# Gated DeltaNet in a fused encoder layer: a 64-row inverse applied twice, front results in DRAM, two fronts per inverse, loads and stores in program order

## The chip, the cores and the metric

The kernel runs on one core of one Trainium2 chip. The metric is the device time of one execution in microseconds (us). All matrices are float32; the large products are made from two exact parts of each operand (a rounded high part and a low rest), three matmuls for one product.

## The reference, cut to what matters

One layer: RMS norm of 1104 tokens (16 meta tokens, 64 of a sample stream, 1024 of a prompt), an input projection of 2048 to 8208 columns, two mixers, an output projection, the residual and a final norm. The mixer that the change touches is the gated DeltaNet, 8 heads of 128, in chunks:

```python
kk = einsum('nbhid,nbhjd->nbhij', kc * bc[..., None], kc) * decay
a_mat = where(strict, kk, 0.0) + eye
t_mat = triangular_solve(a_mat, eye, left_side=True, lower=True, unit_diagonal=True)
u = einsum('nbhij,nbhjd->nbhid', t_mat, vc * bc[..., None])
w = einsum('nbhij,nbhjd->nbhid', t_mat, kc * (bc * exp(gc))[..., None])
# per chunk, in order
v_new = u_i - einsum('bhcd,bhde->bhce', w_i, s)
o = einsum('bhcd,bhde->bhce', q_i * exp(g_i)[..., None], s) + einsum('bhij,bhje->bhie', qk_i, v_new)
s = s * exp(g_last)[..., None, None] + einsum('bhcd,bhce->bhde', k_i * exp(g_last[..., None] - g_i)[..., None], v_new)
```

## The kernel before

The tokens lie in three pieces of 336, 384 and 384 columns. The input projection goes through 64 tiles of 128 output channels, one *job* each. For a tile the weights come in four *chunks* of 256 KB (`Weights`: `load` on the SyncE queue into `wr`, `split` into `wh` on ScalarE and `wl` on VectorE); a chunk feeds 36 matmuls, four groups of nine (three pieces, three products), all into the PSUM tiles `pj`. The first 24 jobs take one piece each; the other 56 take all three pieces, in the order of the string `order` (L416): `b0` is the four tiles (K, Q, V, Z) of head 0, `a2` four tiles of the other mixer. After a tile its convolution, SiLU and gate go on beside the next tile (`convs`), and K, Q, V and Z of a head go to scratch tensors `scr` in DRAM.

The DeltaNet runs beside the projections too. Its unit is three chunks of 128 tokens of one head, 24 units in all, each with a *front* and a *back*. `dn_front` (L717) loads K and Q, transposes them on TensorE (`psq`, `psk`) for the norms, forms the decays, and makes with three matmuls `psm` the masked triangle `bm` and the attention `at`. It stores `bm` to `e_in`; GpSimd loads the twelve 32x32 blocks on the diagonals as 12 rows of `eT`, inverts them with 30 pairs of TENSOR_TENSOR (L792, L794), stores them to `e_out` and loads them back as `t32`. `dn_back` (L803) joins two and two blocks of 32 to 64 (`psx`, `psy`), then the two of 64 to one inverse of 128 (the 64x64 matmuls named `psy2`, `psx2`, `psy3` in the code; they stand as psy and psx with 64*64 in the rows), transposes the values (`psv`), and then takes the three chunks in order: `psr` (keys times state), `r` on VectorE, `psu` (inverse times r), `u` on ScalarE, `psn` (the new state), two matmuls into `po`, `sn` on VectorE. At the end the norm, a transpose (`pot`), the gate, and a store to `yscr`.

The order of the program follows a planner: `clk` adds up the work of TensorE, VectorE and ScalarE, and after each group of nine matmuls `pump` (L182) takes one stage more of whatever is ready; each `yield` gives the planned wait until the next stage. An inverse is planned at `EL` = 5 + 50 of the planner's us. VectorE runs in the order in which the program is written; a scheduler sets the order of the other engines and of the SyncE queue. Every queue takes its instructions strictly in order, so a DMA that waits for its data holds what stands behind it. All matmuls of the helper `mm` have line L83, all VectorE and ScalarE work of the wrapper `Timed` L61.

## Time and profile before

| | us |
|---|---|
| median of 3 runs | 2288.12 |
| lowest and highest run | 2285.22, 2289.0 |
| span of the profiled execution | 2283.8 |
| TensorE busy in that span | 2211.3 (97%) |
| VectorE, ScalarE, GpSimd busy | 1335.5, 640.1, 940.4 |

The profiled execution gives its span from the first to the last instruction; the runs' times hold in addition what lies around it, so the median stands 4.3 us above the span. The profile's page says first how long each engine was busy; then, slice by slice, where; then the chain of work that ended last. A busy share of 97% says that most of what can be won is work taken off TensorE or the little time in which it waits.

### The profile page before, as it was taken

The page shows a single profiled execution, that of the slowest core. Times are in us where ns is not written, and L with a number is a line of the kernel's source. Part 1 is how long each engine was busy: PE and PEld are TensorE (multiplying, and loading weights), DVE is VectorE, ACT ScalarE, POOL GpSimd, SP SyncE. Part 2 cuts the span into 40 slices and gives each one's busy share as a digit, 9 for nine tenths or more (in the row PEclk, how much of TensorE's full clock was granted, in tenths as well). Part 3 has the DMA queues.
Part 4 walks back from the last instruction along what each step waited for, and adds up shares of the span by engine and source line. Part 5 has one row for each costly group of instructions (what it writes and reads, how often), then busy time and mean ns, then how long its engine had stood idle before and what let it go on. Part 6 is the DMA issues. An engine that isn't in the chain of part 4 may idle for free.

```text
span 2283.8 us, 36007 instructions
## 1 busy us (share of the span) xinstructions
PE 2211.3 (97%) x12938; PEld 2074.7 (91%) x12938; DVE 1335.5 (58%) x3421; ACT 640.1 (28%) x1575; POOL 940.4 (41%) x1557
## 2 busy tenths in 40 slices
PE   7799999999999999999999999999999999999998
PEld 6699889999999999999999999999999997788886
DVE  7964355667576547655664567456645345464544
ACT  5443122222222222222222222122222125444341
POOL 4520006657466645555665666655464300000000
PEclk9999999999999999999999999999999999999999
DMA  6444223232323222322222222222222238654652
GB/s 224 148 154 142 64 65 90 69 95 70 91 84 91 71 76 81 97 64 77 80 78 73 79 81 86 73 61 83 86 80 63 62 97 279 216 192 153 217 175 83
DMA packets 168790, 242.69 MB, mean 106 GB/s; under 512 B 18332, under 2 KB 92260, under 8 KB 168484
## 3 DMA queue, kind: packets, MB, share of 16 engines
q1 hardware_dynamic: 163076, 228.84, 32.1%
q0 software_dynamic: 3072, 7.11, 1.7%
q10 hardware_dynamic: 2464, 4.46, 0.5%
q8 instruction: 101, 1.65, 0.3%
q14 instruction: 77, 0.63, 0.1%
HBM read 196.14 MB, written 44.17 MB: 105 GB/s over the span
## 4 chain that ended last, share of the span: by engine, by line
PE 82%; DVE 11%; DMA 2%; issue 2%; ACT 2%; POOL 0%; SPq 0%; DVEq 0%; ACTq 0%; POOLq 0%
PE pj L83 58%; PE po L83 16%; DVE acc L61 2%; PE psy L83 2%; DVE wl L61 2%; DMA yr<-yscr 1%; PE psx L83 1%; PE psm L83 1%; PE psn L83 1%; PE pjb L83 1%; PE psu L83 1%; PE psr L83 1%; ACT jk L61 1%; DVE rot L61 1%; DVE xl L61 1%
## 5 line engine op out<-in xcount | busy, mean ns | idle before, releaser
L83 PE MATMUL pj<-xh,wh 128*128 128x384 f32 x2048 | 692.9, 338 | 8.0 <-DVE raw L61 3.5
L83 PE MATMUL pj<-xl,wh 128*128 128x384 f32 x2048 | 690.6, 337 | 1.1 <-DVE xl L61 1.1
L83 PE MATMUL pj<-xh,wl 128*128 128x384 f32 x2048 | 690.5, 337 | 0.5 <-DVE wl L61 0.4
L61 DVE TENSOR_TENSOR wl<-wr,wh 128x512 fp32r<-128x512 f32 x496 | 371.2, 753 | 343.3 <-ACT wh L61 341.7
L83 PE MATMUL pj<-x,wh 128*128 128x320 f32 (+3 forms) x2048 | 530.6, 340 | 9.4 <-ACT x L61 6.5
L61 ACT CAST wh<-wr 128x512 fp32r<-128x512 f32 x496 | 305.3, 618 | 719.1 <-PE pj L83 522.8
L792 POOL TENSOR_TENSOR tm<-eT 12x30 f32<-12x30 f32 (+4 forms) x720 | 392.1, 545 | 127.3 <-DMA eT<-e_in 72.8
L794 POOL TENSOR_TENSOR eT<-eT,tm 12x30 f32<-12x30 f32 (+4 forms) x720 | 418.5, 581 | 56.4
L83 PEld LDWEIGHTS pj<-xh,wh 128*128 128x128 f32 x2048 | 385.4, 188 | 12.7 <-issue 4.0
L83 PEld LDWEIGHTS pj<-xl,wh 128*128 128x128 f32 x2048 | 385.1, 188 | 2.1 <-DVE xl L61 1.7
L83 PEld LDWEIGHTS pj<-xh,wl 128*128 128x128 f32 x2048 | 384.9, 188 | 1.4 <-DVE wl L61 1.4
L83 PEld LDWEIGHTS pj<-x,wh 128*128 128x128 f32 x2048 | 353.7, 193 | 21.1 <-ACT x L61 6.5
L83 PE MATMUL pj<-x,wl 128*128 128x320 f32 (+3 forms) x1024 | 324.0, 316 | 11.0 <-DVE wl L61 10.9
L83 PE MATMUL po<-wh,yh 128*128 128x512 f32 x656 | 238.9, 396 | 2.6 <-DVE yh L61 1.9
L787 POOL DMA_DIRECT2D eT<-e_in x24 | 17.1, 711 | 504.6 <-DMA e_in<-bm 318.9
L83 PE MATMUL po<-wl,yh 128*128 128x512 f32 x528 | 208.9, 396 | 1.9 <-DVE wl L61 1.9
L83 PEld LDWEIGHTS pj<-x,wl 128*128 128x128 f32 x1024 | 196.9, 192 | 13.7 <-DVE wl L61 13.7
L1058 POOL TENSOR_TENSOR hres<-hres,fw 128x512 f32<-128x512 f32 x1 | 1.7, 1732 | 481.4 <-ACT hres L61 481.4
L83 PEld LDWEIGHTS po<-wh,yh 128*128 128x128 f32 x656 | 123.2, 188 | 34.0 <-ACT wh L61 3.1
L61 DVE SCALAR_TENSOR_TENSOR acc<-raw,pk,acc 128x384 f32<-128x384 f32 (+1 forms) x216 | 147.5, 683 | 5.8
L83 PE MATMUL po<-wh,yl 128*128 128x512 f32 x336 | 132.8, 395 | 0.0
L83 PEld LDWEIGHTS po<-wl,yh 128*128 128x128 f32 x528 | 99.1, 188 | 27.7 <-DVE wl L61 4.1
(254 smaller groups left out, 2191.3 us busy)
## 6 DMA issues: line engine op xcount, KB each, us to landing
wr<-in_w_in SPq DMA_DIRECT2D x320, 256.0 KB, 3.1
wr<-in_w_out SPq DMA_DIRECT2D x176, 256.0 KB, 2.7
scr<-acc SPq DMA_DIRECT2D x48, 192.0 KB, 1.9
kq<-scr SPq DMA_DIRECT2D x48, 192.0 KB, 3.0
hres<-in_x_prompt SPq DMA_DIRECT2D x32, 256.0 KB, 5.3
xr<-in_hT SPq DMA_DIRECT2D x16, 384.0 KB, 4.2
yr<-yscr SPq DMA_DIRECT2D x32, 192.0 KB, 3.4
scr<-co SPq DMA_DIRECT2D x24, 192.0 KB, 1.9
```

Of the source, the lines that this page charges most:

```text
L61: return fn(out, *a, **k)
L83: T.matmul(out, lhsT, rhs, start=start, stop=stop)
L787: G.dma_start(eT, blocks(e_in[i]))
L792: G.tensor_tensor(t, eT[:, j + 1:32, j:j + 1].to_broadcast([12, n, j]), eT[:, j:j + 1, 0:j].to_broadcast([12, n, j]), ALU.mult)
L794: G.tensor_tensor(eT[:, j + 1:32, 0:j], eT[:, j + 1:32, 0:j], t, ALU.add)
L1058: G.tensor_tensor(o, o, fw[:r, ns], ALU.mult)
```

## The change

It does five things. (1) The back stops at the two inverses of 64 rows; `psy2`, `psx2` and `psy3` go. In their place each chunk applies the 64-row inverses (now `ti`), adds the part of the lower left 64x64 block (`b64`) to the lower half of `r`, and applies them again: three `psu` per chunk where there was one. (2) The front stores what the back needs (`knd`, `kmd`, `btd`, `atd`, `qsd`) to DRAM, and the back loads it again, together with K, the inverses (`tn`) and two 32x32 blocks per chunk; the buffers of `kq`, `kn`, `at` and `bm` go from two to one per side, and fronts may run up to six units ahead. (3) One inverse on GpSimd takes the blocks of two fronts: 24 rows instead of 12, 12 times instead of 24; it also writes the ones on the diagonal. It is planned at 5 + 40. (4) The SyncE queue keeps the order of the program while the DeltaNet runs. (5) In `order`, `b7` goes ahead of `a5`.

```diff
-    e_in, e_out = ([dram.tile([1, 61952], F32, tag=f"{n}{i}", name=f"{n}{i}") for i in range(2)]
+    e_in, e_out = ([dram.tile([1, 61952], F32, tag=f"{n}{i}", name=f"{n}{i}") for i in range(6)]
...
+    knd, atd, qsd = ([dram.tile([P, 3, P], F32, tag=f"{n}{i}", name=f"{n}{i}") for i in range(NG)]
+                     for n in ("knd", "atd", "qsd"))
+    btd = [dram.tile([64, 3, 64], F32, tag=f"btd{i}", name=f"btd{i}") for i in range(NG)]
+    kmd = [dram.tile([P, P], F32, tag=f"kmd{i}", name=f"kmd{i}") for i in range(NH)]
...
-    t32 = [const([P, 3, P], f"t32_{i}") for i in range(2)]
...
-    fronts, backs, el_done, front_of, state = [0], [0], {}, {}, {}
+    state, scales, inv_done, pool_free = {}, {}, {}, [0.0]
...
-    pool_free = [0.0]
...
     def pump():
-        while True:
+        moved = True
+        while moved:
...
-            f, b = fronts[0], backs[0]
-            if "gate" in done and "front" not in running and f < NG and f - b <= 1:
-                h, p = divmod(f, 3)
-                if (KQ, h, p) in done and (QQ, h, p) in done:
-                    running["front"] = [0.0, dn_front(h, p)]
-            if "back" not in running and b < f and b < NG and el_done.get(b, 1e9) <= clk["pe"]:
-                h, p = divmod(b, 3)
-                if (VQ, h, p) in done and (ZQ, h, p) in done:
-                    running["back"] = [0.0, dn_back(h, p)]
...
-                        if k == "back":
-                            backs[0] += 1
-                        elif k == "front":
-                            fronts[0] += 1
-            if not moved:
-                break
...
-            yield
...
+        if p:
+            yield
...
-    order = "b0 b1 b2 b3 a2 b4 a3 b5 a4 b6 a5 b7 a6 a7"
+    order = "b0 b1 b2 b3 a2 b4 a3 b5 a4 b6 b7 a5 a6 a7"
...
+    net.enter_context(tc.manual_schedule(engines={mybir.EngineType.SP}))
...
-    EL = (5.0, 50.0)
-    for i in range(2):
-        V.memset(t32[i], 0.0)
-        Q.dma_start(whole(e_out[i]), t32[i])
+    b32 = dn.tile([P, 3, P], F32, tag="b32", name="b32")
+    b64 = dn.tile([P, 3, P], F32, tag="b64", name="b64")
+    V.memset(b32, 0.0)
+    V.memset(b64, 0.0)
+    for e in e_out:
+        Q.dma_start(whole(e), b32)
+    def part(t, r, c, n):
+        return bass.AP(t.tensor, t.offset + 416 * r + c, [[416, n], [4448, 3], [1, n]])
...
     def dn_front(h, p):
-        kq = tmp("kq", "kq", 2, (P, 3, 2, P))
+        f = 3 * h + p
+        kq = tmp("kq", "kq", 1, (P, 3, 2, P))
...
-        yield 2.1
+        yield 4.0
...
+        kn = tmp("kn", "kn", 1)
+        V.tensor_tensor(kn, pk_[:, 0:3, :], kds[:, h, c3, None].to_broadcast([P, 3, P]), ALU.mult)
+        Q.dma_start(knd[f], kn)
+        if p == 0:
+            km = dn.tile([P, P], F32, tag="km", name="km")
+            V.tensor_scalar(km, pk_[:, 0, :], kdm[:, h:h + 1], None, ALU.mult)
+            Q.dma_start(kmd[h], km)
+        yield 0.3
...
-        cq = dn.tile([P, 12], F32, tag="cq", name="cq", bufs=2)
+        cq = scales[f] = dn.tile([P, 12], F32, tag="cq", name="cq", bufs=6)
...
-        kn = tmp("kn", "kn", 2)
-        V.tensor_tensor(kn, pk_[:, 0:3, :], kds[:, h, c3, None].to_broadcast([P, 3, P]), ALU.mult)
-        km = None
-        if p == 0:
-            km = dn.tile([P, P], F32, tag="km", name="km")
-            V.tensor_scalar(km, pk_[:, 0, :], kdm[:, h:h + 1], None, ALU.mult)
...
-        bm = tmp("bm", "bm", 2)
+        bm = tmp("bm", "bm", 1)
...
-        at = tmp("at", "at", 2)
+        at = tmp("at", "at", 1)
...
+        bt = tmp("bt", "bt", 1, (64, 3, 64))
...
+            V.tensor_tensor(bt[:, c, :], pm[0:64, 0, 64:P], at[0:64, c, 64:P], ALU.mult)
...
-        yield 1.4
-        eT = dn.tile([12, 32, 32], F32, tag="eT", name="eT", bufs=1)
-        i = (3 * h + p) % 2
-        Q.dma_start(whole(e_in[i]), bm)
-        G.dma_start(eT, blocks(e_in[i]))
-        tm = dn.tile([12, 240], F32, tag="tm", name="tm", bufs=1)
+        V.tensor_tensor(kq[:, :, 1, :], kq[:, :, 1, :], gr, ALU.mult)
+        yield 0.2
+        Q.dma_start(whole(e_in[f % 6]), bm)
+        Q.dma_start(btd[f], bt)
+        Q.dma_start(atd[f], at)
+        Q.dma_start(qsd[f], kq[:, :, 1, :])
+    def inverse(g):
+        eT = dn.tile([24, 32, 32], F32, tag="eT", name="eT")
+        sl = [(2 * g + i) % 6 for i in range(2)]
+        for i, e in enumerate(sl):
+            G.dma_start(eT[12 * i:12 * i + 12], blocks(e_in[e]))
+        G.memset(eT.rearrange("m a b -> m (a b)")[:, 0:1024:33], 1.0)
+        tm = dn.tile([24, 240], F32, tag="tm", name="tm")
...
-            G.tensor_tensor(t, eT[:, j + 1:32, j:j + 1].to_broadcast([12, n, j]),
-                            eT[:, j:j + 1, 0:j].to_broadcast([12, n, j]), ALU.mult)
+            G.tensor_tensor(t, eT[:, j + 1:32, j:j + 1].to_broadcast([24, n, j]),
+                            eT[:, j:j + 1, 0:j].to_broadcast([24, n, j]), ALU.mult)
...
-        G.dma_start(blocks(e_out[i]), eT)
-        G.dma_start(t32[i], whole(e_out[i]))
-        yield 0.3
-        V.tensor_tensor(kq[:, :, 1, :], kq[:, :, 1, :], gr, ALU.mult)
-        front_of[h, p] = (kq, kn, km, at, cq, bm)
-        pool_free[0] = el_done[3 * h + p] = max(clk["pe"] + EL[0], pool_free[0]) + EL[1]
+        for i, e in enumerate(sl):
+            G.dma_start(blocks(e_out[e]), eT[12 * i:12 * i + 12])
+        pool_free[0] = inv_done[g] = max(clk["pe"] + EL[0], pool_free[0]) + EL[1]
+    EL = (5.0, 40.0)
+    def dn_fronts():
+        for f in range(NG):
+            h, p = divmod(f, 3)
+            while f % 2 == 0 and f - backs[0] > 4:
+                yield 1.0
+            while not {(KQ, h, p), (QQ, h, p)} <= done:
+                yield 1.0
+            yield from dn_front(h, p)
+            if f % 2:
+                inverse(f // 2)
+    def dn_backs():
+        for f in range(NG):
+            h, p = divmod(f, 3)
+            while f // 2 not in inv_done or not {(VQ, h, p), (ZQ, h, p)} <= done:
+                yield 1.0
+            if inv_done[f // 2] > clk["pe"]:
+                yield inv_done[f // 2] - max(clk.values())
+            yield from dn_back(h, p)
+            backs[0] += 1
...
     def dn_back(h, p):
-        kq, kn, km, at, cq, bm = front_of.pop((h, p))
+        f = 3 * h + p
+        cq = scales.pop(f)
+        tn = tmp("tn", "tn", 1)
+        Q.dma_start(tn, whole(e_out[f % 6]))
+        for r in (32, 96):
+            Q.dma_start(b32[r:r + 32, :, r - 32:r], part(e_in[f % 6], r, r - 32, 32))
...
-        tn = t32[(3 * h + p) % 2]
-        V.tensor_tensor(tn, tn, cst[:, None, C_ID:C_ID + P].to_broadcast([P, 3, P]), ALU.add)
+        kq = tmp("kq", "kqb", 1, (P, 3, 2, P))
+        Q.dma_start(kq[:, :, 0, :], scr[h][KQ][p].rearrange("p (c t) -> p c t", t=P))
+        Q.dma_start(b64[0:64, :, 64:P], btd[f])
+        kn = tmp("kn", "knb", 1)
+        Q.dma_start(kn, knd[f])
+        if p == 0:
+            km = dn.tile([P, P], F32, tag="kmb", name="km")
+            Q.dma_start(km, kmd[h])
+            s = dn.tile([P, P], F32, tag="s", name="s0", bufs=2)
+            Q.dma_start(s, s_delta[h])
+            state[h] = s
+        at = tmp("at", "atb", 1)
+        Q.dma_start(at, atd[f])
+        Q.dma_start(kq[:, :, 1, :], qsd[f])
+        yield 4.0
...
-        b32 = tmp("b32", "b32", 1)
-        V.tensor_tensor(b32, bm, cst[:, None, C_M32:C_M32 + P].to_broadcast([P, 3, P]), ALU.mult)
...
-        tt = tmp("tt", "tt", 1)
-        V.tensor_tensor(tt, ti, py[:, 0:3, :], ALU.add)
-        py2 = psd("psy2")
-        for c in range(3):
-            mm(py2[:64, c, 0:64], x[0:64, c, 0:64], tn[0:64, c, 0:64], True, True)
-        t64 = tmp("t64", "t64", 1, (64, 3, 64))
-        V.tensor_tensor(t64, tn[0:64, :, 0:64], py2[0:64, 0:3, 0:64], ALU.add)
-        yield 0.3
-        px2 = psd("psx2")
-        for c in range(3):
-            mm(px2[0:64, c, 0:64], bm[64:128, c, 0:64], tt[64:128, c, 64:128], True, True)
-        y64 = b32[0:64, :, 0:64]
-        S.copy(y64, px2[0:64, 0:3, 0:64])
-        yield 0.3
-        py3 = psd("psy3")
-        for c in range(3):
-            mm(py3[0:64, c, 0:64], t64[:, c, :], y64[:, c, :], True, True)
-        S.copy(tt[0:64, :, 64:128], py3[0:64, 0:3, 0:64])
+        V.tensor_tensor(ti, ti, py[:, 0:3, :], ALU.add)
...
-        if p == 0:
-            s = dn.tile([P, P], F32, tag="s", name="s0", bufs=2)
-            Q.dma_start(s, s_delta[h])
-            state[h] = s
-            yield 2.5
-        else:
-            yield 0.3
+        yield 0.3
...
-            mm(pu[:, 0, :], tt[:, c, :], r, True, True)
+            mm(pu[:, 0, :], ti[:, c, :], r, True, True)
+            u = dn.tile([P, P], F32, tag="u1", name="u1", bufs=1)
+            S.copy(u, pu[:, 0, :])
+            yield 1.05
+            pu = psd("psu")
+            mm(pu[:, 0, :], b64[:, c, :], u, True, True)
+            V.scalar_tensor_tensor(r[64:128], pu[64:128, 0, :], cq[64:128, 9 + c:10 + c], r[64:128], ALU.mult,
+                                   ALU.add)
+            yield 0.25
+            pu = psd("psu")
+            mm(pu[:, 0, :], ti[:, c, :], r, True, True)
...
+    backs = [0]
+    running["front"] = [0.0, dn_fronts()]
+    running["back"] = [0.0, dn_backs()]
...
-    while "front" in running or "back" in running or backs[0] < NG:
+    while running:
```

How this moves instructions. TensorE, one chunk in a back of head 0 (`u_5806` is the first product, `b_3219` is `b64`; rows of `pj` left out). Before:

```order
L83 MATMUL psr<-sn,kq 128x128
...
L83 MATMUL psu<-r,tt 128x128
...
L83 MATMUL psn<-u,kn 128x128
L83 MATMUL po<-u,at 128x128
L83 MATMUL po<-sn,kq 128x128
```

and with the change:

```order
L83 MATMUL psr<-sn,kq 128x128
...
L83 MATMUL psu<-r,ti 128x128
...
L83 MATMUL psu<-u_5806,b_3219 128x128
...
L83 MATMUL psu<-r,ti 128x128
...
L83 MATMUL psn<-u,kn 128x128
L83 MATMUL po<-u,at 128x128
L83 MATMUL po<-sn,kq 128x128
```

Two matmuls of 128x128 are new in each chunk, each behind a result of ScalarE or VectorE; here nine `pj` matmuls stand between any two of them, as before.

TensorE in the back before that one, a place at which the next front (`psq`, `psk`) falls between, with the change:

```order
L83 MATMUL psu<-r,ti 128x128
L83 MATMUL pj_5211<-x_351,wh 128x336 x2
L87 MATMUL psq<-cst,kq 128x128 x3
L83 MATMUL psu<-u_5166,b_3219 128x128
L87 MATMUL psk<-cst,kq 128x128 x3
L83 MATMUL psu<-r,ti 128x128
L83 MATMUL psn<-u,kn 128x128
```

Here the chain of one chunk stands almost without `pj` between its steps. Before the change no `psu` has fewer than nine `pj` behind it until `psn`.

The SyncE queue where a back begins (`wr` is a chunk of weights). Before, the third unit of head 1:

```order
L231 DMA wr<-in_w_in 128x512
L721 DMA kq<-scr_83 128x3x128
L721 DMA kq<-scr_86 128x3x128
L231 DMA wr<-in_w_in 128x512
L806 DMA vT<-scr_79 128x384
L916 DMA yscr_183<-zg 128x384
L231 DMA wr<-in_w_in 128x512 x2
```

and with the change, the first unit of head 2:

```order
L953 DMA yscr_184<-zg 128x384
L840 DMA tn<-e_out_210 128x3x128
L842 DMA b_3218<-e_in_204 32x3x32 x2
L844 DMA vT<-scr_89 128x384
...
L849 DMA kn<-knd_222 128x384
...
L857 DMA at<-atd_246 128x384
L858 DMA kq<-qsd_270 128x3x128
L720 DMA kq<-scr_96 128x3x128
...
L720 DMA kq<-scr_99 128x3x128
L723 DMA gr<-gscr 128x384
L220 DMA wr<-in_w_in 128x512
```

Before, at most seven other DMAs stand between two chunks of weights; now ten or more stand there in 26 places, sixteen in this one, and twenty in the longest.

## Rows read from the trace of the kernel before

**Rows 1.** The page, busy us, share of the span and instructions of each engine.

```profile
PE 2211.3 (97%) x12938; PEld 2074.7 (91%) x12938; DVE 1335.5 (58%) x3421; ACT 640.1 (28%) x1575; POOL 940.4 (41%) x1557
```

**Rows 2.** Busy time by stretch: length, PE, PEld, DVE, ACT, POOL, clock, DMA share, GB/s.

```profile
300.00:1855.00 1555.00, 1532.47 (x9636) 1489.51 (x9636) 923.24 (x2649) 363.40 (x1047) 863.71 (x1512) 1.00 0.27 78
```

**Rows 3.** Waits of PE, 300 to 1860 us: waited for, total us, times, longest.

```profile
PE pj L83 <- DVE raw L61: 3.5, 2, 1.9
...
PE pj L83 <- DVE wl L61: 3.0, 3, 1.7
PE psq L87 <- DMA s<-in_s_delta: 2.4, 1, 2.4
PE psu L83 <- DVE r L61: 2.1, 5, 0.7
```

**Rows 4.** Timeline of PE, 1144 to 1162 us: start, duration, instruction.

```profile
1144.84 0.83 PE L83 MATMUL psx<-ti,b 128*128 128x128 f32 x6
...
1147.04 0.83 PE L83 MATMUL psy<-x,t 128*128 128x128 f32 x6
...
1149.99 0.56 PE L83 MATMUL psx<-tt,bm 64*64 64x64 f32 x6
...
1152.19 0.56 PE L83 MATMUL psy<-b,t 64*64 64x64 f32 x6
1152.67 0.55 PE L87 MATMUL psv<-cst,vT 128*128 128x128 f32 x3
...
1154.57 0.47 PE L83 MATMUL pj<-x,wh 128*128 128x336 f32 x2
...
1156.07 0.47 PE L83 MATMUL pj<-x,wh 128*128 128x336 f32 x2
...
1159.65 0.38 PE L83 MATMUL psu<-r,tt 128*128 128x128 f32 x2
...
1161.43 0.38 PE L83 MATMUL psn<-u,kn 128*128 128x128 f32 x2
```

**Rows 5.** Timeline of all engines, 1157 to 1161 us, one chunk's steps.

```profile
1157.67 0.43 PE L83 MATMUL psr<-s,kq 128*64 128x128 f32 x2
1158.14 0.34 DVE L61 SCALAR_TENSOR_TENSOR r<-psr,cq,vb 64x128 f32<-64x128 f32 x1 [1.46 <-PE psr L83]
...
1160.07 0.27 ACT L61 COPY u<-psu 128x128 f32<-128x128 f32 x1 [4.82 <-PE psu L83]
```

**Rows 6.** Groups of DVE: 300 to 1860 us, then the last from 171 to 300.

```profile
L61 DVE TENSOR_TENSOR wl<-wr,wh 128x512 fp32r<-128x512 f32 x215 | 165.6, 770 | 116.5 <-ACT wh L61 116.4
...
L61 DVE TENSOR_TENSOR t<-t,cst 128x384 f32<-128x384 f32 x24 | 14.6, 607 | 0.0
...
L61 DVE SCALAR_TENSOR_TENSOR r<-psr,cq,vb 64x128 f32<-64x128 f32 x8 | 2.7, 343 | 5.4 <-PE psr L83 5.2
...
L61 DVE TENSOR_TENSOR wl<-wr,wh 128x512 fp32r<-128x512 f32 x42 | 28.8, 690 | 45.7 <-ACT wh L61 45.5
```

**Rows 7.** POOL: timeline of one inverse, then its largest form at the end.

```profile
1139.04 0.70 POOL L787 DMA_DIRECT2D eT<-e_in  x1 [11.21 <-DMA e_in<-bm]
...
1183.46 0.72 POOL L795 DMA_DIRECT2D e_out<-eT  x1 [0.30 <-POOL eT L794]
1187.77 0.78 POOL L796 DMA_DIRECT2D t<-e_out  x1 [3.59 <-DMA e_out<-eT]
...
L1058 POOL TENSOR_TENSOR hres<-hres,fw 128x512 f32<-128x512 f32 x1 | 1.7, 1732 | 481.4 <-ACT hres L61 481.4
```

**Rows 8.** The SyncE queue: one issue; size and us to landing; a chunk on PE.

```profile
1135.50 0.39 SPq L786 DMA_DIRECT2D e_in<-bm  x1
...
wr<-in_w_in SPq DMA_DIRECT2D x215, 256.0 KB, 3.0
...
759.40 5.97 PE pj L83 x36
```

**Rows 9.** Busy time by stretch, where the DeltaNet begins (columns as rows 2).

```profile
330.00:336.00 6.00, 4.78 (x22) 4.81 (x23) 1.84 (x10) 2.83 (x13) 0.00 (x0) 0.72 0.55 170
```

**Rows 10.** The chain that ended last, after the last back: start, us, what.

```profile
1852.12 24.23 PE pj L83 x147
```

## The prediction

> **What bounds the kernel now.** I read the page's engine shares first. TensorE is busy for 2211.3 of 2283.8 us [rows 1], so work on other engines counts only where TensorE waits for it or where it delays something TensorE waits for. Then busy time by stretch: the DeltaNet runs from about 300 to 1855 us, and there TensorE is busy for 1532 of 1555 us, at the full clock of 2.4 GHz, with VectorE at 923 and GpSimd at 864 us [rows 2]. Then TensorE's waits in that stretch: sixteen kinds, some 22 us in all, the largest 3.5 us [rows 3]. So at most 22 us lie in waits, and everything else is matmul work. The change touches this stretch alone; the 428 us behind it are taken as they are. Last, the chain around the end of the DeltaNet: after the last back TensorE goes straight on with the last tile for 24 us [rows 10]; it never waits there for a back to end. That backs end earlier (in the new order fourteen weight chunks are still to be loaded after the last one, where it was one) is therefore worth nothing.
>
> **Matmul work that goes and comes.** The timeline prices it [rows 4]. Nine plain matmuls take 1156.07 - 1154.57 = 1.50 us. Between the starts of psx and psy, 1144.84 and 1147.04, stand three 128x128 and nine plain ones: 2.20 - 1.50 = 0.70, or 0.233 each. From psy to the 64x64 psx, 2.95 us, are three more of them, three of 64x64 and nine plain: 2.95 - 1.50 - 0.70 = 0.75 for the three small ones. The next three: 1152.19 - 1149.99 - 1.50 = 0.70. The last three: 0.48 until psv starts. A small matmul thus costs nearly as much as a large one. Removed per back 0.75 + 0.70 + 0.48 = 1.93, times 24: 46 us. A lone psu costs 1161.43 - 1159.65 - 1.50 = 0.28. Two per chunk are added, 144 in all: 34 us at 0.233, 40 at 0.28; I take 0.25, since some stand side by side: 36. **Work: -10 us**, between -6 and -12.
>
> **The longer chain of a chunk.** Each chunk gets two more turns: psu to ScalarE's u to psu, and psu to VectorE's r to psu. One turn over ScalarE ends 1160.34 - 1159.65 = 0.69 us after psu's start, 0.44 of it after psu's own 0.25; one over VectorE ends 1158.48 - 1157.67 = 0.81 after the start [rows 5]. Nine plain matmuls hide either. Before, five of 72 psu stand closer, and they are the five waits of 2.1 us in all [rows 3]: 0.42 each, and the other 67 never wait. So the price is read off the new order: where fewer than nine stand between. I count 19 such steps behind VectorE, 24 behind ScalarE, and 5 from psx to psy. At 0.42 the 19 cost 8; those behind ScalarE can cost 0.44 at most, where nothing stands between (three do), about 3 together; psx to psy, 5 times 0.4, 2. Less the 2.1 of before: **+11 us**, between +3 (VectorE free, as in rows 5) and +18 (all 48 at 0.42). Where the scheduler has moved the DeltaNet's matmuls together, TensorE has nothing else to do, and whoever is late next is VectorE.
>
> **VectorE and GpSimd.** Removed per back: the identity (0.61), the mask and the small add; added: three updates of half r at 0.34 [rows 6] and three small products per front. That is even within 10 us over 1555 and beside other work; its cover is VectorE's idle 40%. Half of GpSimd's pairs go. This matters through VectorE: with GpSimd at work wl takes 770 ns, without it 690, over 215 of them 17 us [rows 6]. If all of VectorE is slowed by such a tenth, half of 90 us comes back, and of TensorE's waits for VectorE (some 13 us of the 22) perhaps a quarter. **-3 us**, between 0 and -10. The Trainium skill, "SBUF — State Buffer", section "Who interferes with whom", says that a VectorE instruction with two SBUF inputs contends with a GpSimd instruction that reads SBUF and that the loser blocks; by it the sum would move towards the first rival below.
>
> **The inverse.** Its path from the store of bm to the reload runs from 1135.50 to 1187.77, 52.3 us [rows 7, 8], and a second load issue adds 0.7. In the new order the tightest backs (five of 24) ask for their inverse eight weight chunks after that store: 8 times 5.97 [rows 8] is 47.8, with the DeltaNet's matmuls among them 50 to 60. So SyncE waits 0 to 3 us there, three times. 24 rows instead of 12 should cost no more: a 128x512 form takes 1732 ns [rows 7], so the price goes by columns. I put 0 to +4.
>
> **The queue.** New per unit are five or six stores and six to eight loads, all on SyncE. A weight chunk is now queued when TensorE starts the chunk two before it, 2 times 5.97 = 12 us ahead [rows 8], and the DeltaNet's own matmuls add one or two. Ten issues at about 0.4 [rows 8], some 4 us of waits for the gate's result and for a store to land, and 3.0 to landing: 11 us. This fits; sixteen or twenty do not quite. I put **+1**, between 0 and +25 (a us late at each of the 26 places). At the beginning six zero stores replace two; there TensorE waits 2.4 us for the first K and Q [rows 3] and the clock is granted at 0.72 afterwards [rows 9]. Psq stands some 2.5 us later in the new order, so I leave this even, between -3 and +4.
>
> **The sum.** -10 + 11 - 3 + 0 + 1 = -1; with the even terms rounded down, -2: a span of 2281.8 and, at 4.3 above it, **2286 us** against the median of 2288.1. One term of work is given back by the chain. I call 0.2%, 4.6 us, the least that a measurement of this kernel can tell from no change. This case's own range is 2279 to 2293.
>
> **Rivals.** *The chain is hidden, and VectorE gains more.* The scheduler put the DeltaNet's matmuls together where it thought weights late, and if VectorE is freed by half of GpSimd's time, r is there when asked for. For it: 67 of 72 steps never wait now. Against it: the seven rows in which a whole chunk stands with two plain rows. Then -10 for the work stays, and up to 10 of the 22 us of waits go: 2268, from 2262 to 2281. Chance 0.28.
>
> *The queue holds the weights (slower).* SyncE in program order stands before a store until VectorE has made its data, and every weight chunk behind it stands too; wl is then late, and since VectorE also runs in program order, r behind it is late as well. The place is the start of each back, the price 1 us at each of 26 places, more at the bursts of sixteen and twenty: some +25, 2311. It decides when a chunk lands more than about 12 us after the one two ahead has begun. For it: the sum above for sixteen issues is already there. Against it: TensorE lost only 3.0 us to wl before. The Trainium skill, "DMA: Bandwidth & Descriptors", section "Anatomy of one DMA", has the rule on which it rests: a semaphore wait "happens on the issuing sequencer before dispatch", and about 2.0 us of a DMA is fixed. The landing time of 3.0 us agrees; that a waiting store delays weights here no row of before shows. Chance 0.22.
>
> *The inverse takes longer with 24 rows.* If it took twice its 40 us, SyncE would stand 35 us at five places with weights behind it, and TensorE, with 12 us in hand, some 23 at each: +115, 2400. The 1732 ns speak against it. Chance 0.03. That the change doesn't do what it says can be set aside: the order shows half the GpSimd pairs and two psu more per chunk; 0.02 for no effect at all.
>
> **Chances.** The forecast has 0.45: 0.30 within 0.2%, 0.09 below it, 0.06 above. The first rival adds 0.28 to faster, the queue 0.22 and the inverse 0.03 to slower, the last 0.02 to same. Faster 0.37, same 0.32, slower 0.31. The range of 2264 to 2308 leaves out the ends of the two main rivals and the long inverse, under 0.2 together.
>
> **What would show it.** Right: the nine small matmuls gone, psu at 432 records where it had 144; GpSimd's pairs at half the time, each as long as now; wl in the DeltaNet nearer 700 than 770 ns; waits of psu and psn for r and u of some 10 to 13 us in total, at the close places alone; TensorE's busy time down by 10 us or so. The queue's rival shows as waits of pj for wl, or of ScalarE for weights, well over 3 us behind the start of backs. The forecast is wrong if TensorE's waits in the DeltaNet come to under 15 us or over 45.

## The result and the profile after

The changed kernel takes 2371.26 us (median of 4 runs, 2369.11 to 2372.72); the kernel before, beside it, 2286.67. The ratio is 1.037 [1.0355, 1.0385]: **slower by 84.6 us**, where 2286 was forecast. The span of the profiled execution is 2370.4, 86.6 more than before. The page's row of the engines; then, by stretch, the whole DeltaNet with most of what is left of the projection behind it, and three stretches of 57 us (columns as rows 2):

```profile
PE 2236.7 (94%) x12794; PEld 2104.3 (89%) x12794; DVE 1306.0 (55%) x3493; ACT 642.2 (27%) x1599; POOL 505.0 (21%) x825
```

```profile
300.00:1935.00 1635.00, 1549.90 (x9449) 1510.03 (x9448) 890.80 (x2717) 364.83 (x1070) 428.15 (x780) 0.98 0.34 98
...
456.00:513.00 57.00, 49.78 (x281) 47.35 (x279) 42.30 (x131) 13.93 (x43) 35.02 (x64) 0.91 0.36 107
1596.00:1653.00 57.00, 48.21 (x270) 45.40 (x268) 40.97 (x118) 15.61 (x53) 35.61 (x65) 0.91 0.40 121
1083.00:1140.00 57.00, 57.00 (x368) 56.59 (x367) 25.15 (x71) 9.60 (x26) 0.00 (x0) 1.00 0.25 72
```

TensorE is busy 25 us longer than before [rows 1] with 144 records fewer, so that it was not given more to do: the granted clock fell to 0.91 where it waits, and stayed at 1.00 in [rows 2]. From 1083 to 1140 us no front runs, only backs with their three psu per chunk, and there it is busy all the time. Its waits from 300 to 1960 us add up to 84.9 us at 71 places; before, 26.6 at 33. The largest (columns as rows 3):

```profile
PE psq L87 <- DMA kq<-scr: 20.5, 16, 4.2
PE pj L83 <- DVE wl L61: 19.4, 10, 4.1
PE pj L83 <- DVE zr L61: 11.7, 5, 3.2
PE pot L87 <- DVE on L61: 10.4, 4, 2.9
PE psu L83 <- DVE r L61: 8.2, 11, 1.7
```

(`zr` and `on` are VectorE's first step behind a tile of Z and the normed output of a back.) So 58 us of the 87 are waits. Over the whole execution the mean granted clock fell from 0.993 to 0.979; 0.014 of 2370 us is 33 us, so the clock can account for the other 28. The first kind of wait, psq for K and Q, came to 1.3 us before. Its cause stands in two timelines: the kernel before (a load of K and Q on SyncE, and its psq), then the changed kernel.

```profile
627.94 1.19 SPq L721 DMA_DIRECT2D kq<-scr  x2
...
638.62 0.49 PE L87 MATMUL psq<-cst,kq 128*128 128x128 f32 x3
```

```profile
618.17 0.57 SPq L792 DMA_DIRECT2D qsd<-kq  x1
620.91 1.21 SPq L720 DMA_DIRECT2D kq<-scr  x2
...
624.74 0.55 PE L87 MATMUL psq<-cst,kq 128*128 128x128 f32 x3 [4.22 <-DMA kq<-scr]
```

Before, the load was issued 10.7 us ahead of psq; now 3.8, and all of that is wait: TensorE stood at psq from 620.5, before the load was issued. Over all 24 fronts this lead was 5.5 to 21.3 us before, 10.6 in the median; now it is 3.5 to 6.3, 4.5 in the median, for two loads that are issued one behind the other and take 3.1 us each to land. With one buffer, the load must wait until the store of q~ (`qsd`, q times its decay) out of that buffer has landed (31.2 us of SyncE's time at 14 places, up to 3.9), and in program order it cannot go ahead of anything. TensorE, VectorE and ScalarE then stand behind one another. The timeline of all engines around a later pair of fronts:

```profile
1603.13 0.52 PE L87 MATMUL psq<-cst,kq 128*128 128x128 f32 x3 [0.29 <-DMA kq<-scr]
...
1607.58 0.28 ACT L61 ACTIVATE jk<-po 128x128 bf16<-128x128 f32 x1
...
1607.98 0.53 DVE L61 TENSOR_TENSOR so<-so,cq 128x3 f32<-128x3 f32 x1 [5.60 <-ACT jk L61]
...
1613.24 0.56 DVE L61 TENSOR_TENSOR on<-po,roy 128x384 f32<-128x384 f32 x1
...
1613.86 0.55 PE L87 MATMUL pot<-cst,on 128*128 128x128 f32 x3 [2.92 <-DVE on L61]
```

ScalarE's squares of a back's output (jk from po) are queued behind those of a front's psq and psk; VectorE stands 5.6 us for them, then needs 5.3 us of small steps until `on`, and TensorE waits for that. Two parts of the forecast did come: VectorE is relieved, and 24 rows cost what 12 did (groups by line, of the changed kernel; at 12 rows the two pair steps took 581 and 545 ns):

```profile
L61 DVE TENSOR_TENSOR wl<-wr,wh 128x512 fp32r<-128x512 f32 x213 | 153.0, 718 | 148.9 <-ACT wh L61 148.3
...
L807 POOL TENSOR_TENSOR eT<-eT,tm 24x30 f32<-24x30 f32 (+4 forms) x360 | 202.1, 561 | 28.2
L805 POOL TENSOR_TENSOR tm<-eT 24x30 f32<-24x30 f32 (+4 forms) x360 | 192.5, 535 | 27.3
```

### The profile page after: what moved, and what is told of

Same layout as the page of the kernel before. It is cut to its first block, busy times and chain, and to the rows that moved or that the text cites. A ratio compares the mean times of both kernels' runs of the same rounds, so it can differ in the third digit from the quotient of the medians.

```text
span 2370.4 us, 35527 instructions
## 1 busy us (share of the span) xinstructions
PE 2236.7 (94%) x12794; PEld 2104.3 (89%) x12794; DVE 1306.0 (55%) x3493; ACT 642.2 (27%) x1599; POOL 505.0 (21%) x825
## 4 chain that ended last, share of the span: by engine, by line
PE 69%; DVE 14%; DMA 8%; issue 3%; SPq 3%; ACT 3%; POOL 0%; DVEq 0%; ACTq 0%; POOLq 0%
PE pj L83 47%; PE po L83 15%; DMA wr<-in_w_in 2%; DVE wl L61 2%; PE psu L83 2%; DMA kq<-scr 2%; DVE acc L61 1%; ACT jk L61 1%; DMA yr<-yscr 1%; DMA qsd<-kq 1%; DVE rqt L61 1%; DVE at L61 1%; DVE bm L61 1%; DVE rqy L61 1%; PE pjb L83 1%
## 5 line engine op out<-in xcount | busy, mean ns | idle before, releaser
L83 PE MATMUL pj<-xh,wh 128*128 128x384 f32 x2048 | 701.9, 343 | 14.3 <-DVE zr L61 11.7
L83 PE MATMUL pj<-xl,wh 128*128 128x384 f32 x2048 | 699.1, 341 | 0.0
L83 PE MATMUL pj<-xh,wl 128*128 128x384 f32 x2048 | 698.1, 342 | 0.3 <-DVE wl L61 0.2
L61 DVE TENSOR_TENSOR wl<-wr,wh 128x512 fp32r<-128x512 f32 x496 | 360.4, 730 | 381.2 <-ACT wh L61 379.1
L83 PEld LDWEIGHTS pj<-xh,wh 128*128 128x128 f32 x2048 | 391.5, 191 | 18.6 <-DVE zr L61 12.8
L83 PEld LDWEIGHTS pj<-x,wh 128*128 128x128 f32 x2048 | 359.3, 196 | 19.8 <-ACT x L61 6.6
L83 PE MATMUL pj<-x,wl 128*128 128x320 f32 (+3 forms) x1024 | 329.7, 322 | 29.8 <-DVE wl L61 29.8
L807 POOL TENSOR_TENSOR eT<-eT,tm 24x30 f32<-24x30 f32 (+4 forms) x360 | 202.1, 561 | 28.2
L805 POOL TENSOR_TENSOR tm<-eT 24x30 f32<-24x30 f32 (+4 forms) x360 | 192.5, 535 | 27.3
L61 DVE SCALAR_TENSOR_TENSOR acc<-raw,pk,acc 128x384 f32<-128x384 f32 (+1 forms) x216 | 134.8, 624 | 6.2
L83 PEld LDWEIGHTS po<-wl,yh 128*128 128x128 f32 x528 | 99.1, 188 | 26.6 <-DVE wl L61 2.9
```

The costliest lines, as they stand in the source:

```text
L61: return fn(out, *a, **k)
L83: T.matmul(out, lhsT, rhs, start=start, stop=stop)
L805: G.tensor_tensor(t, eT[:, j + 1:32, j:j + 1].to_broadcast([24, n, j]), eT[:, j:j + 1, 0:j].to_broadcast([24, n, j]), ALU.mult)
L807: G.tensor_tensor(eT[:, j + 1:32, 0:j], eT[:, j + 1:32, 0:j], t, ALU.add)
```

## The experiments

Times are medians; the ratio is to the kernel before on the same chip; the last column is the sum of TensorE's waits from 300 to 1960 us (26.6 before, 84.9 in the change).

| run | us | ratio [95%] | waits |
|---|---|---|---|
| e1_auto_queue | 2360.41 | 1.0315 [1.0292, 1.0337] | 83.3 |
| e3_raw3 | 2357.74 | 1.031 [1.029, 1.033] | 75.9 |
| e5_weights_act_queue | 2371.27 | 1.0362 [1.0336, 1.0389] | 88.9 |
| e4_inverse_alone | 2329.84 | 1.0187 [1.0167, 1.0207] | 60.6 |
| e6_order_alone | 2287.73 | 1.0004 [0.9991, 1.0017] | 26.0 |
| e7_part1_and_order | 2334.74 | 1.0216 [1.0198, 1.0233] | 64.6 |
| e22_part1_shorter_plan | 2314.81 | 1.0118 [1.0101, 1.0135] | 53.3 |
| e8_two_kq | 2361.19 | 1.0333 [1.0314, 1.0351] | 81.5 |
| e9_later_stages | 2387.69 | 1.0435 [1.0407, 1.0463] | 102.0 |
| e10_one_front_per_inverse | 2435.47 | 1.0652 [1.063, 1.0673] | 128.2 |
| e13_unpaired_auto_queue | 2460.37 | 1.0767 [1.0747, 1.0788] | 164.3 |
| e14_unpaired_auto_near | 2391.04 | 1.046 [1.0443, 1.0478] | 107.4 |
| e16_auto_queue_two_kq | 2344.11 | 1.0251 [1.0236, 1.0266] | 68.7 |
| e17_fronts_asked_later | 2352.39 | 1.03 [1.0276, 1.0324] | 77.9 |
| e18_later_auto_two_kq | 2331.98 | 1.02 [1.0182, 1.0218] | 74.2 |
| e20_fronts_beside_no_tail | 2323.61 | 1.0155 [1.0138, 1.0173] | 61.1 |
| e21_auto_no_tail | 2298.38 | 1.005 [1.0035, 1.0065] | 46.3 |
| e25_longer_inverse_plan | 2304.46 | 1.0079 [1.0065, 1.0094] | 47.3 |

### Is it the queue of the weights?

Two theories to begin with: Q, the weights stand on SyncE; C, the chain of a chunk is too long. E1 takes the program's order off SyncE, E3 gives the raw weights a third buffer (`(wpool, "w", (2, 2))` becomes `(3, 2)`), E5 issues the weights on ScalarE's queue while the DeltaNet runs.

```diff
# e1
-    net.enter_context(tc.manual_schedule(engines={mybir.EngineType.SP}))
# e5
-            Q.dma_start(wr, self.specs[self.n_load])
+            (nc.scalar if scr_on[0] else Q).dma_start(wr, self.specs[self.n_load])
```

> The changed kernel without the line that keeps SyncE in program order; all else stays. Theory Q (weights stand on SyncE behind DeltaNet transfers that wait for their data): the scheduler may put the weights ahead again, so most of the 84 us goes: 2280 to 2315 us, TensorE's waits for wl in the DeltaNet under 8 us (30 now). Theory C (the longer chain of a chunk and the matmuls pushed together): nothing goes, 2355 us or more.

> The changed kernel with three buffers instead of two for weights as they are loaded, so that a chunk is queued three chunks ahead of its use and not two. Theory Q: the wait for wl falls to a third or less and the time to 2295 to 2340 us; what is left are waits for K and Q and for the gate. Theory C: no change, 2365 to 2375 us.

> The changed kernel with the weights of the projection issued from ScalarE's queue while the DeltaNet runs; SyncE keeps program order for all the rest. Theory Q: 2280 to 2315 us, waits for wl under 8 us, while waits for K and Q stay. Theory C: 2355 us or more.

E1 and E3 give back 11 and 14 us, E5 nothing; wl's waits are 17.8, 19.7 and 21.1 us, where theory Q asked under 8 of E1 and E5. Off SyncE, the weights' loads no longer stand behind the DeltaNet's transfers, and yet wl is as late as before; the waits of E5:

```profile
PE psq L87 <- DMA kq<-scr: 29.9, 16, 4.1
PE pj L83 <- DVE wl L61: 21.1, 11, 4.1
```

E5 alone would leave a doubt, since ScalarE, which now issues the loads, also makes `wh`. The changed kernel's own timeline settles it:

```profile
1609.81 0.62 ACT L61 CAST wh<-wr 128x512 fp32r<-128x512 f32 x1 [1.86 <-PE pj L83]
...
1625.72 0.68 DVE L61 TENSOR_TENSOR wl<-wr,wh 128x512 fp32r<-128x512 f32 x1
...
1626.45 0.63 PE L83 MATMUL pj<-x,wl 128*128 128x320 f32 x1 [3.23 <-DVE wl L61]
```

The weights had landed and `wh` was done at 1610.4; VectorE came to `wl` 15.3 us later, busy for 14.5 of them, above all with the norm of a back and the small steps and masks of a front. At all ten waits for wl, `wh` was done 3.5 to 15.3 us before `wl` began. So it is VectorE, and not the place of the weights in SyncE's queue, that makes wl late, and Q falls as the main cause. E3's time lies between its two ranges; why the third buffer gives 14 us is not shown. C is tried next.

### Part 1 and the order, on the kernel before

E4 is the kernel before with the 64-row inverses applied twice (the back's and the front's edits of part 1; the inverses stay per front and in SBUF); E6 has `b7` ahead of `a5` alone, E7 both, E22 in addition `EL = (5.0, 44.0)`.

> The kernel before with the first part of the change alone: three psu per chunk, the 64-row inverse applied twice, psy2, psx2 and psy3 gone; fronts, inverses, buffers and queue as before. Theory Q: my term for it, -10 us of work and some +5 to +11 of close places: 2276 to 2295 us. Theory C: the chain alone costs most of the 84 us: 2340 us or more.

> The kernel before with part 5 alone (b7 ahead of a5). Theory T (the tail: the extra 43 us of the run with part 1 alone come from backs that overrun the projection) has nothing to say against the order itself: 2283 to 2292, waits of TensorE in the DeltaNet at 20 to 35 us, and the last back earlier by some 100 us. Rival O (the order itself costs, since the DeltaNet's work is pushed together and the last tiles of the other mixer come late): 2300 or more.

> The kernel before with part 1 (64-row inverses applied twice) and part 5 (b7 ahead of a5). Theory T: without the overrun at the end part 1 costs what its matmuls and its chain cost, -10 to +12 us against the order alone, so 2278 to 2305, and the waits of 38 us behind 1860 us are gone. Rival C (the longer chain costs in the whole DeltaNet): 2315 to 2335, with waits of psu for r and u of over 25 us.

> The kernel before with parts 1 and 5, and the inverse planned at 5 + 44 instead of 5 + 50, so that a unit, 65.8 us long in that run where it was 60.6, is planned shorter and DeltaNet ends before the projection. Theory T: what part 1 cost was the overrun alone; the last pot comes before 1880 and the time is 2275 to 2297. Rival I (the path of an inverse takes 52 us whatever the plan says, so SyncE holds the weights at every reload): 2300 to 2345, waits of TensorE for wl or psx of over 25 us ahead of 1850.

The order costs nothing, but it does not bring the last back forward either (1855.0 us, before 1851.8, where some 100 us were expected). Part 1 costs 47 us in this frame (E7 against E6; E4, without the order, is 42 us above the kernel before and between its two ranges), and the new order does not cure it. E7's time lies in rival C's range, but its waits of psu and psn for r and u, 13.6 us, are far from the 25 that C asked. Of E7's waits 34.0 us lie before 1850 us (E6: 21.8) and 30.5 behind (E6: 4.2). Busy time by stretch behind 1850, E6 and then E7 (columns as rows 2), and then E7's waits there:

```profile
1850.00:1930.00 80.00, 78.43 (x386) 67.26 (x385) 39.83 (x94) 31.10 (x77) 0.00 (x0) 1.00 0.66 207
```

```profile
1850.00:1930.00 80.00, 50.91 (x246) 44.16 (x244) 24.09 (x69) 12.00 (x39) 20.42 (x38) 0.70 0.16 47
```

```profile
PE pot L87 <- DVE on L61: 10.6, 2, 5.7
PE psx L83 <- DVE b L61: 10.3, 1, 10.3
```

The first and the last pot stand at 456.9 and 1855.0 in E6, at 465.1 and 1908.7 in E7. With 23 units between, a unit takes 60.8 us there and 62.8 here (the 65.8 in E22's expectation was too high). At most two units are in flight, so a longer unit delays all that follow; the last one runs when every tile of the projection but one is done, alone and at a clock of 0.70. The DRAM stores of part 2 and the fronts far ahead take this limit away: in the change the last pot stands at 1865.4, and the projection goes on to 1965. E22 ends at 1880.0 and has no tail (2.3 us of waits behind 1850), but now 51.0 us ahead of it, for on, r and b. Neither of its theories holds: the overrun makes 26 of the 39 us by which E7's waits exceed E6's, and a shorter plan buys it off with waits elsewhere, still 27 us above E6. Part 1 without either price was not measured.

### Fronts: pairs, buffers, lead

E8 gives the fronts' K and Q a second buffer; E9 plans 9 instead of 4 behind the loads of fronts and backs. E10 makes one inverse of 12 rows per front; E13 is E10 with E1's edit; E14 is E13 with fronts at most three units ahead.

```diff
# e8
-        kq = tmp("kq", "kq", 1, (P, 3, 2, P))
+        kq = tmp("kq", "kq", 2, (P, 3, 2, P))
# e9, in dn_front and dn_back
-        yield 4.0
+        yield 9.0
# e10
-            while f % 2 == 0 and f - backs[0] > 4:
+            while f - backs[0] > 4:
...
-            if f % 2:
-                inverse(f // 2)
+            inverse(f)
# e14
-            while f - backs[0] > 4:
+            while f - backs[0] > 2:
```

> The whole change with two buffers for the fronts' K and Q instead of one. Theory L (a front's load of K stands behind the landing of the store of q~ of the front before it, 3 us and more, and psq is asked for too early): the 20.5 us of psq's waits fall under 8, the time by 15 to 30 us with the clock that comes back, 2341 to 2356. Rival S (SyncE in program order is late with everything in the bursts, so that the load lands late all the same): psq's waits stay at 15 to 22, 2364 to 2373.

> The whole change with planned waits of 9 instead of 4 behind the loads of a front and of a back. Theory L: the matmuls are placed too early for loads that take two trips through DRAM; one more chunk of weights between hides them: psq's waits under 8 us and those of the weights under 20, 2335 to 2356. Rival V (VectorE, in the order of the program, is held in the bursts by ScalarE's squares and by stores, whatever the loads do): the waits move but do not shrink by more than 10 us, 2360 to 2378.

> The whole change with part 3 undone: one inverse of 12 rows per front, as before, planned at 5 + 40; all else as in the change. Theory P (pairs: two fronts close together, with backs beside them, ask VectorE and ScalarE for too much in one place): the waits of psq, pot, zr and wl shrink to half, 2325 to 2345. Rival R (the round trip through DRAM and the order of the stages cost, however the fronts are spaced): 2360 to 2380, with GpSimd's busy time back at some 900 us.

> The change with parts 3 and 4 undone: one inverse per front, and the scheduler's order on SyncE. Theory P: the 10 us that the queue's order gave come on top, 2310 to 2335. Rival R: what the queue alone gave, 2350 to 2365.

> As the run with parts 3 and 4 undone, with fronts at most three units ahead of the backs (two in the kernel before, five in the change), so that fronts and backs take turns as before and only the work of parts 1 and 2 is left. Theory P: close to before, 2285 to 2310, TensorE's waits under 40 us. Rival R: waits stay over 70 us, 2345 to 2365, above all those of psq for K and Q.

The pairs do not explain the loss: without them it is 64 us worse, above both ranges that were set for E10, and the lead of K and Q is as short (4.4 us in the median). What the 64 us are is not shown. E13 and E14 also lie above all their ranges, but they cannot say what parts 1 and 2 cost: they plan each inverse of 12 rows at 5 + 40, where its path took 52.3 us [rows 7, 8], and SyncE, in the scheduler's order, stands for its reload, in E13 for 89.2 us at 8 places and in E14 at nearly every unit:

```profile
SPq L838 <- DMA e_out<-eT: 161.3, 23, 20.8
```

A second buffer alone (E8) gives 10 us, between its two ranges, and leaves psq 17.5 us of waits, because in program order the load still goes out only 5 us ahead. E9 is worse than both of its ranges, but its waits have changed kind:

```profile
PE psx L83 <- DVE ti L61: 24.8, 13, 4.7
PE psu L83 <- DVE r L61: 20.1, 17, 4.9
...
PE psq L87 <- DMA kq<-scr: 1.2, 2, 0.8
PE pj L83 <- DVE wl L61: 1.2, 4, 0.6
```

The median lead is 7.3 us. psq's waits go from 20.5 to 1.2, and wl's from 19.4 to 1.2 with them; others come, for ti and r, and E17 puts them down to the longer wait of the *backs*: without it ti falls to 4.2 and r to 9.2 us. That gave theory H: what is lost is the lead of the loads of K and Q. E16 is E1 and E8 together; E17 is E9 for fronts alone; E18 is all three.

> The change with part 4 undone and two buffers for the fronts' K and Q. In the kernel before, the loads of K and Q are issued 10 to 11 us ahead of psq (448.16 to 458.85, 570.84 to 580.45); in the change 4 to 4.5 us (598.66 to 603.13). Theory H (the lead of the loads is what is lost: one buffer and the program's order both take it): only when both are undone does the scheduler hoist them, lead 8 us and more, psq's waits under 6 us, 2325 to 2348. Rival A (each of the two gave its 10 us by itself): 2350 to 2356, with psq's waits over 12 us.

> The whole change with a planned wait of 9 instead of 4 behind the loads of a front; the back's stays 4. Theory H: a lead of 9 to 11 us; psq's waits under 3 us, and since VectorE no longer stands for ScalarE's squares of a late psq, the waits for wl and zr fall under half too (31 to under 15), 2325 to 2350. Rival B (VectorE's bursts are the cause and psq only their first sign): psq's waits go, but those for r, on, wl and ti rise by as much, 2360 to 2390, as when both waits were made longer.

> Both at once: planned wait of 9 behind a front's loads, the scheduler's order on SyncE, two buffers for the fronts' K and Q. Theory H: nothing is left of the waits for K and Q; whatever waits remain have another cause. 2315 to 2340, and 2300 or less only if the waits for on, r and wl go with them. Rival B: 2355 or more.

Buffer and order together give 27 us, as theory H asked and more than the 11 and 10 of each, psq's waits fall to 3.6; E17 gives 19, just outside its range, with psq at 2.4 and wl at 3.7; E18 gives 39. So some 40 of the 85 us come back with the lead, and with what else its three edits move. Little of that shows as waits:

```profile
PE 2211.5 (95%) x12794; PEld 2093.1 (90%) x12794; DVE 1311.3 (56%) x3493; ACT 642.5 (28%) x1599; POOL 510.5 (22%) x825
```

E18's span is 35 us shorter than the change's, TensorE's busy time 25 and its waits 11; but they come at 38 places instead of 71. How much of the 25 is the clock is not shown, since its mean rose only from 0.979 to 0.981. In E18 these waits are left:

```profile
PE pj L83 <- DVE wl L61: 19.5, 5, 10.0
PE pot L87 <- DVE at L61: 13.7, 3, 6.5
...
PE pot L87 <- DVE on L61: 8.0, 4, 3.0
```

### Fronts beside the ends of backs

One of the three for `at`, in E18's timeline:

```profile
1588.88 0.33 DVE L61 SCALAR_TENSOR_TENSOR sn<-sn,egl,psn 128x128 f32<-128x128 f32 x1
1589.14 1.97 DVE L61 SCALAR_TENSOR_TENSOR bm<-gr,gc,cst 128x128 f32<-128x128 f32 x3
...
1593.77 0.57 DVE L61 TENSOR_TENSOR so<-so,cq 128x3 f32<-128x3 f32 x1
...
1599.35 0.56 DVE L61 TENSOR_TENSOR on<-po,roy 128x384 f32<-128x384 f32 x1
...
1600.76 0.66 PE L87 MATMUL pot<-cst,on 128*128 128x128 f32 x2 [6.45 <-DVE at L61]
```

Between the state's last step and `on` stand a front's masks and the norm of a back: with the front's small steps ahead of them, VectorE is busy for 16.0 of the 17 us from 1583 to 1600, almost three weight chunks long (5.97 each [rows 8]). E20 (on E17) and E21 (on E18) keep the two apart:

```diff
# dn_fronts
+            while "tail" in state:
+                yield 0.5
+            state["front"] = 1
             yield from dn_front(h, p)
+            del state["front"]
# dn_back, ahead of the norm
+        while "front" in state:
+            yield 0.5
+        state["tail"] = 1
...
         done.add(("y", 8 + h, p))
+        del state["tail"]
```

> The whole change with the wait of 9 behind a front's loads, and no front beside the end of a back: a front waits until a back that is in its norm and gate is done, and a back waits ahead of its norm until the front is done. Theory V (what the late loads leave is the collision of a front's VectorE work, 14 short steps and nine passes, with the norm of a back, 14 more, within some three weight chunks): the waits of pot for on and at fall from 22 us to under 8, 2318 to 2340. Rival N (they are the price of the longer way whatever stands beside it): 2345 to 2365.

> The same on top of the scheduler's order on SyncE and two buffers for the fronts' K and Q (2332 without it). Theory V: pot's 22 us fall under 8; 2305 to 2322, with the 10 us wait for wl at 436, where the reload of an inverse stands ahead of a weight chunk, left over. Rival N: 2326 to 2340.

Theory V holds: pot's waits fall from 22 us to 3.5 and 3.4, and E20 is 29 us faster than E17 (though psu's waits for r rise there from 9.2 to 17.4), E21 34 faster than E18 and below its range. E21 is 1.005 [1.0035, 1.0065] against the kernel before: 73 of the 85 us are undone, with parts 1, 3 and 5 in place, and part 2 but for one buffer. Its row of the page:

```profile
PE 2203.2 (96%) x12794; PEld 2087.1 (91%) x12794; DVE 1299.6 (57%) x3493; ACT 641.0 (28%) x1599; POOL 514.9 (22%) x825
```

TensorE is busy 8.1 us less than before [rows 1], at a mean granted clock of 0.986 where it was 0.993: here the work that part 1 takes off it can be seen. What E21 has left is one thing above all (SyncE's waits from 300 to 500 us, then the timelines of SyncE and of TensorE):

```profile
SPq L843 <- DMA e_out<-eT: 14.1, 1, 14.1
```

```profile
427.28 0.37 SPq L843 DMA_DIRECT2D tn<-e_out  x1
...
429.02 0.38 SPq L220 DMA_DIRECT2D wr<-in_w_in  x1
```

```profile
434.22 0.64 PE L83 MATMUL pj<-x,wl 128*128 128x324 f32 x1 [10.01 <-DVE wl L61]
```

The reload of the first inverse stands 14.1 us ahead of a weight chunk: here the rival of the queue is real. The Trainium skill, "DMA: Bandwidth & Descriptors", section "Anatomy of one DMA", says that a semaphore wait "happens on the issuing sequencer before dispatch"; this row agrees. In E18 it is so twice: SyncE stands 48.6 us at three reloads, and behind two of them, at 428 and 1512 us, TensorE waits 10.0 and 6.5 us for wl. It comes with the scheduler's order (E1: 50.3 us at five reloads); in the changed kernel SyncE never waits for an inverse. E25 plans the inverse at 5 + 46 and puts waits of 1.0 and 0.5 into the front's VectorE work:

> The run without fronts beside ends of backs (2298), with the inverse planned at 5 + 46 instead of 5 + 40 and short planned waits of 1.0 and 0.5 inside a front's VectorE work, where it was one stretch of 10 us. Theory V with the reload: the 10 us wait for wl at 434, where the reload of the first inverse stands ahead of a weight chunk, is gone, and those for raw and zr (5 us each, behind a front's VectorE stretch) shrink: 2278 to 2292. Rival: the waits move to other places, 2293 to 2305.

```profile
PE psu L83 <- DVE r L61: 17.5, 15, 3.5
PE pj L83 <- DVE wl L61: 9.8, 2, 9.5
```

This missed: a 9.5 us wait is still there, r's doubled (8.8 to 17.5), and the time, 2304.46, is in the rival's range. No run here beats the kernel before. SyncE's program order on the kernel before by itself was not measured.

## Why the prediction was wrong

- **The step that failed is the queue's term, "I put +1".** It asked only whether a *weight* chunk lands late, and counted ten issues against 12 us. What lands late are the new unit's own K and Q: their lead fell from 10.6 to 4.5 us in the median, since one buffer makes the load wait for a store and the program's order keeps it where it is written. The buffers' "two to one" stood in the change and had no term. psq's waits alone are 20.5 us; with the lead given back, 39 us go (E18). That psq "stands some 2.5 us later", taken as a help, was argued for the first front alone.
- **VectorE's term, "its cover is VectorE's idle 40%", failed too.** The sum of its work was not the fault (1306.0 us busy in the whole execution, against 1335.5 in [rows 1]), but cover is a matter of place: fronts, which no longer take turns with backs, meet the norm of a back within two or three chunks. Keeping them apart gives 34 us more (E21).
- **The clock was left out.** 58 us of added waits came with 87 of added span; the waits' bounds were priced at the full clock.
- **The chain, +11**, was about the right size in the changed kernel, as far as its own waits show: psu and psn wait 9.8 us for r and u (the shown 8.2 is the most of it), where 10 to 13 were expected and 2.1 stood before. In the frame of before it costs more, by a path that the prediction did not have: with two units in flight a longer unit delays all that follow, and the room behind the last back is only some 24 us [rows 10]. The remark that backs which end earlier are worth nothing has no test here: with the order alone (E6) they do not end earlier.
- **The inverse, 0 to +4**, held: 561 and 535 ns for the two steps of a pair at 24 rows, and in the changed kernel SyncE never waits for it. Where SyncE waits for it by more than 1.5 us in all, the run has the scheduler's order (50.3 us in E1, 48.6 in E18, 14.1 in E21).
- **GpSimd's relief, -3**, held in kind: wl takes 718 ns instead of 770 [rows 6], as the Trainium skill, "SBUF — State Buffer", section "Who interferes with whom", would have it. No gain of TensorE's from it can be seen.
- **The work, -10**, can't be read off the changed kernel's busy time, since the clock moved it. In E21, where most waits are gone, TensorE is busy 8.1 us less than before, so the term looks right.
- **The queue's rival** had the sign and the place right, but named weights and 25 us; in the changed kernel `wh` was done before each late wl, so its mechanism is not what happened there. The sign of being wrong that was set, waits under 15 or over 45 us, came true with 84.9.

## What to carry to other kernels

When a change halves a buffer or fixes a queue's order, look up how far ahead of its use each load is issued now, and charge every load whose lead falls below its landing time and the store it has to wait for. An engine that is idle 40% of the time may cover nothing where two bursts meet: compare the work between two deadlines, not over the stage. And where a few units are in flight, a longer unit costs nothing until the last one outlives the work that hides it.

## What the runs showed of the hardware

In the two stretches of 57 us with a granted clock of 0.91, TensorE has two long waits each, of 2.6 and 3.2 us and of 2.9 and 3.2 us. Stretches of 3 us in the first of them show what follows its wait of 2.6 us, which ended at 487.3: full speed up to 486, the lower level of 1.2 GHz from 489 to 492 although TensorE is busy again, and full speed once more:

```profile
483.00:486.00 3.00, 1.66 (x10) 1.33 (x9) 2.69 (x10) 0.62 (x1) 2.62 (x5) 1.00 0.01 3
...
489.00:492.00 3.00, 3.00 (x11) 3.00 (x11) 2.79 (x9) 0.00 (x0) 2.69 (x5) 0.50 0.36 131
492.00:495.00 3.00, 3.00 (x18) 2.86 (x17) 2.76 (x11) 0.00 (x0) 2.68 (x5) 0.98 0.00 0
```

Where TensorE has little to do, E7's busy time by stretch shows the lower level through a whole stretch, and the full 2.4 GHz while the last tile of the projection runs:

```profile
1860.00:1880.00 20.00, 4.18 (x25) 3.15 (x23) 6.96 (x22) 1.97 (x9) 11.44 (x25) 0.68 0.13 32
1880.00:1900.00 20.00, 14.83 (x49) 11.37 (x49) 3.71 (x10) 1.81 (x6) 0.00 (x0) 0.50 0.04 10
...
1920.00:1940.00 20.00, 19.21 (x98) 16.78 (x97) 9.06 (x23) 6.75 (x19) 0.00 (x0) 1.00 0.52 170
```

In the changed kernel 87 us of span came with 58 us of added waits at 71 places; in E18, with 38 places, 51 came with 48. So what a microsecond of wait costs beyond itself is not one figure for all runs.
